# A hybrid encoder layer on one Trainium2 core: three instead of two groups of seven products in the second pass of each down projection

## The chip, the cores and the metric

The kernel runs on one core of one Trainium2 chip. The metric is the time of one execution on the device in microseconds, the median of three runs; the profile comes from one profiled execution, recorded by the hardware profiler. Engines are named as the profile names them: PE is TensorE (matmuls; PEld are its weight loads), DVE is VectorE, ACT is ScalarE, POOL is GpSimd, SP is SyncE, which here issues most of the DMAs.

## What is computed

One layer over 256 rows of width 2048, in float32. Two half feed-forward blocks (FFNs) with an inner width of 5632 stand around a mixer (a state-space part and an attention part), and a gated embedding follows:

```python
def swiglu(h, w_gate, w_up, w_down):
    return (jax.nn.silu(h @ w_gate) * (h @ w_up)) @ w_down

x = x + 0.5 * swiglu(rms_norm(x, ffn1_norm[i]), ffn1_w_gate[i], ffn1_w_up[i], ffn1_w_down[i])
...
x = x + mixed @ w_out[i]
x = x + 0.5 * swiglu(rms_norm(x, ffn2_norm[i]), ffn2_w_gate[i], ffn2_w_up[i], ffn2_w_down[i])
gate = jax.nn.sigmoid(rms_norm(x, ple_norm[i]) @ w_ple_gate[i])
```

The change is in the products with `w_down` (5632 x 2048), once in each FFN; the profile calls the weights `in_ffn_w_down`.

## The kernel before

**Arithmetic.** Each float32 operand of a matmul is split into a high part (`hi`, rounded to the type that PE takes in one pass) and a low part (`lo`, the rest). A product is the sum of three: high by high, low by high, high by low. The split of a weight tile of 128 x 1024 (`split`, lines 181 and 184) is a cast on ACT and a subtraction on DVE. Tiles named `whi`/`wlo` and `shi`/`slo` are two rings of buffers for split weights, 4 and 3 deep, used in turn (`weight_pair`, line 285); `hhi`/`hlo` and `nhi`/`nlo` are split activations.

**Tiling of the down projection** (`ffn`, from line 667). The 5632 rows of `w_down` are 11 k blocks (0 to 10) of 512; the 2048 columns are four blocks of 512, worked off as two pairs (`for n in range(0, ND, 2)`). The 256 rows of x are two tiles of 128. For one k block and one pair there are two ways to multiply:

- *A column, `"c"`* (`Seven.column`, line 543): for each of the two column blocks, both row tiles by the four 128-row parts of the k block, 24 matmuls of 512 columns each, 48 in all. Its weights come in two loads of 1 MB and make four splits.
- *A group of seven products, `"s"`* (`Seven.chunk`, line 505): the same four quarter products by seven instead of eight half-size ones (the Winograd form of Strassen's scheme), 7 x 6 = 42 matmuls. It needs sums of the weight quarters: t1, t2 and t4 are DVE additions of 128 x 1024 (line 502), and a fourth sum is made by a DMA issued by POOL that adds one quarter of the weights onto another in place (line 526). It splits seven weight tiles. It also needs sums of the hidden rows, which `sum_forms` (line 450) makes with four small DVE additions (line 459) and one split.

`plans` (line 693) writes out by hand in which order the k blocks of each pair are taken. `"a"` takes all the k blocks that it lists for the first column block, calls `end(0)`, then takes them in reverse order for the second column block and calls `end(1)`. `end` adds the finished sums into x (line 678) and puts off `nxt.block`, which turns that block of x for the next stage. After the last group, `opened` (line 680) adds the parts that are shared by both columns into x.

**Hidden rows.** `kept` (line 699) holds the two k blocks of split hidden rows used last; any other k block is split again when it is needed. `summed` (line 706) holds the sums of k blocks 1 and 2 from the first pair for the second, but not those of k block 0.

**Turned blocks of x.** The next stage needs x transposed. `Normed.block` (line 388) does it for one block of 512 columns: two transposes of 32 x 32 squares on DVE (line 217), 16 small copies on SP's queue (line 230, `h<-mid`), and then `parted`, which multiplies by the norm's gain and splits (lines 192 and 194). The last block of the mixer's norm goes over PE instead.

**What sets the order.** The program is traced in order. Work that stands beside the matmuls is put off by a number of steps with `put_off`; a step is one weight half (or, in a group, two products) of the traced matmuls. The framework then places the instructions of each engine by its own model of their times, an instruction traced earlier going first among those that are ready. So a number of steps sets a rank and is no wait on the chip. Each engine runs its own list in order.

**Buffers.** Weight loads have five buffers of 1 MB; x occupies two of them, so three are left during the down stage. A buffer is free again when its parts are split. Sums of weights and of hidden rows share two buffers (`sum`).

Of the kernel before, what the change touches and what calls it, by code (L numbers as in the profile page):

```python
# [33 lines left out]
def layer_kernel(ctx: ExitStack, tc: tile.TileContext, a: dict, shapes: dict, out: bass.AP):  # L34
# [10 lines left out]
    ND = D // NB  # L45
# [17 lines left out]
    def uid(s):  # L63
        count[0] += 1
        return f"{s}_{count[0]}"
# [4 lines left out]
    def com(tag):  # L70
        return get(comp, tag, *{"sg": (1024, 1), "h": (1024, 2), "sq": (NB, 1), "mid": (2048, 1)}[tag])
# [4 lines left out]
    def aux(s="aux"):  # L76
        return auxp.tile([P, 1024], F32, tag="aux", name=uid(s))
# [4 lines left out]
    def small(n=8):  # L82
        return smp.tile([P, 8], F32, tag="sm", name=uid("sm"))[:, :n]

    def halves(kind):

        return [
            actp.tile([P, 4, T], F32R, tag=kind + s, name=uid(kind + s), bufs={"n": 4, "h": 2}[kind])
            for s in ("hi", "lo")
        ]  # L90
# [4 lines left out]
    def start(g):  # L95
        beside.append(g)
        return g
# [10 lines left out]
    def put_off(steps, fn, *args):  # L108


        def g():
            for _ in range(steps):
                yield
            fn(*args)

        return start(g())

    def pin(ins):
        return tc.keep_in_program_order(ins)
# [58 lines left out]
    def split(hi, lo, src, scale=None, pinned=False):  # L178

        if scale is None:  # L180
            copy = nc.scalar.copy(hi, src)  # L181
            if pinned:
                pin(copy)
            rest = nc.vector.tensor_tensor(out=lo, in0=src, in1=hi.bitcast(F32), op=ALU.subtract)  # L184
            return copy.ins, rest.ins
        else:
            split_each(hi.unsqueeze(1), lo.unsqueeze(1), src.unsqueeze(1), [scale])
# [27 lines left out]
    def turn_blocks(mid, src, t, k0, nk):  # L215

        nc.vector.transpose(
            mid[:, :, t, k0 : k0 + nk, :].rearrange("p q f b -> p f q b"),
            src.rearrange("p (f q b) -> p f q b", f=nk, q=4),
        )  # L220

    def turn_quarters(out, mid, steps):


        def g():
            for _ in range(steps):
                yield
            for i in range(4):
                for q in range(4):
                    nc.sync.dma_start(  # L230
                        out[32 * q : 32 * q + 32].rearrange("p (t i w) -> p t i w", t=TT, i=4)[:, :, i],
                        mid[32 * i : 32 * i + 32, q].rearrange("p t f b -> p t (f b)"),
                    )
                yield

        return start(g())

    def by_tile(out, nk):

        return out.rearrange("p (x f b) -> p f x b", f=nk, b=32)  # L240
# [53 lines left out]
    @contextmanager  # L294
    def sums_phase(name):
        with phase(name) as pool:
            yield pool
            ring[0] = None
# [76 lines left out]
    class Normed:  # L375
# [12 lines left out]
        def block(self, n):  # L388
            if self.laid:
                ps = self.laid(n)  # L390
            elif n < self.early:

                if n % 2 == 0 or self.mid is None:
                    self.mid = com("mid")
                mid = self.mid[:, n % 2 * 1024 : n % 2 * 1024 + 1024].rearrange(
                    "p (q t f b) -> p q t f b", q=4, t=TT, b=32
                )
                out = com("h")
                for t in range(TT):
                    turn_blocks(mid, xt[t][n], t, 0, 4)  # L400
                soon = n == ND - 1
                turn_quarters(out, mid, 4 if soon else 6)
                put_off(9 if soon else 11, self.parted, n, by_tile(out, 4))
                put_off(1, self.squares, n)
                return
            else:
                ps = aux()
                for t in range(TT):
                    for j in range(4):
                        pin(nc.tensor.transpose(  # L410
                            ps[:, j * T + t * P : j * T + (t + 1) * P], xt[t][n][:, j * P : (j + 1) * P], ident
                        ))
            self.parted(n, ps.rearrange("p (j s) -> p j s", j=4))
            if not self.laid:
                put_off(1, self.squares, n)
# [34 lines left out]
    def sum_forms(pool, u, kind="n"):  # L450

        sums = pool.tile([P, 2, NB], F32, tag="sum", name=uid("rows"), bufs=2)
        s = sums.rearrange("p j n -> p (j n)").rearrange("p (z j x b) -> p z j x b", z=4, j=2, b=32)
        (a11, a21), (a12, a22) = ([u[:, k : k + 2, 4 * t : 4 * t + 4] for t in range(TT)] for k in (0, 2))
        for z, (x, y, op) in enumerate((
            (a21, a22, ALU.subtract), (s[:, 0], a11, ALU.subtract),
            (a11, a21, ALU.subtract), (a12, s[:, 1], ALU.add),
        )):
            nc.vector.tensor_tensor(out=s[:, z], in0=x, in1=y, op=op)
        both = halves(kind)  # L460
        split(*both, sums.rearrange("p j n -> p (j n)").rearrange("p (z t) -> p z t", z=4))
        return both
# [95 lines left out]
    def ffn(i, xn, nxt, bg=None):  # L558
# [4 lines left out]
        sevens = pools.enter_context(sums_phase(f"sums{i}"))  # L563
# [20 lines left out]
        for f in range(NF):  # L584
# [6 lines left out]
            if f >= early:  # L591
# [17 lines left out]
                s = Seven(xn, lambda kb: sums[kb], ((wg, f * NB), (wu, f * NB)), sevens, turns)  # L609
# [59 lines left out]
        def rows(k):  # L669
            return hT[k // 2][:, k % 2 * 4 : k % 2 * 4 + 4]  # L670
# [6 lines left out]
        def gather(x, ps, scale):  # L677
            nc.vector.scalar_tensor_tensor(out=x, in0=ps, scalar=scale, in1=x, op0=ALU.mult, op1=ALU.add)

        def opened(s, n):  # L680
# [11 lines left out]

        plans = (
            (("c", 3), ("c", 4), ("s", 0), ("c", 5), ("c", 6), ("s", 1), ("c", 7), ("c", 8), ("s", 2), ("c", 9), ("c", 10)),
            (("c", 10), ("c", 9), ("s", 2), ("c", 3), ("s", 1), ("a", (0, 4, 5, 6, 7, 8))),
        )
        parts, forms = {}, {}

# [12 lines left out]
        for n in range(0, ND, 2):  # L711

            def end(side):
                m = n + side
                for t, z in enumerate(((2, 4), (3, 8))[side]):
                    gather(xt[t][m], s.bank(z), 0.5)
                put_off(0 if m == ND - 1 and m < nxt.early else 2, nxt.block, m)

            s = Seven(kept, summed, ((wd, n * NB), (wd, (n + 1) * NB)), sevens, turns)
            plan = plans[n // 2]  # L720
            left = sum(kind == "s" for kind, _ in plan)
            for kind, kb in plan:
                final = (kind, kb) == plan[-1]
                if kind == "s":
                    left -= 1
                    s.chunk(kb, () if left else shared)
                    if not left:
                        put_off(0, opened, s, n)
                    continue
                for side in range(2):  # L730
                    s.column(side, (kb,) if kind == "c" else kb[:: 1 - 2 * side], final)
                    if final:
                        end(side)
# [694 lines left out]

    n1, nm, n2, npl = Normed("ffn1_norm", load_turned), Normed("mix_norm"), Normed("ffn2_norm", kinds="hhnn", late=0), Normed("ple_norm", late=0)
    ffn(1, n1, nm, s5_prep)  # L1430

    w_in = a["w_in"][0]
# [47 lines left out]
    mix.close()  # L1480

    ffn(2, n2, npl)


# [43 lines left out]
    n = ND - 1  # L1528
# [12 lines left out]
    s = small(1)  # L1541
# [144 lines left out]
```

## Time and profile before

| what | value |
|---|---|
| median of three runs | 1823.55 us (1822.76 to 1824.12) |
| the profiled execution's own time | 1823.55 us |
| its span, first to last instruction | 1821.8 us |
| PE busy, matmuls | 1814.3 us, 8948 |
| DVE busy, instructions | 1523.6 us, 1779 |
| ACT busy, instructions | 1048.4 us, 1223 |
| POOL busy | 102.6 us |
| moved by DMA | 425.79 MB, mean 234 GB/s |

Times in the profile are microseconds from the start of the span; a duration called "ns" is in nanoseconds. A line such as `L184 DVE TENSOR_TENSOR wlo<-raw,whi` names the line of the kernel, the engine, the operation, and what it writes from what it reads, without buffer numbers. In a timeline the first number is the start, the second the duration, and brackets at the end give the idle time ahead of it and what ended that. Many operations belong to helpers, so one line serves all stages; the stage is told by the time.

The down projection of the first FFN lies roughly between 477 and 711 us, that of the second between 1482 and 1714 us. The output projection (`w_out`), which also turns blocks of x, lies ahead of 1030 us.

### The profile page before, as it was taken

The page shows a single profiled execution, that of the slowest core. Times are in us where ns is not written, and L with a number is a line of the kernel's source. Part 1 is how long each engine was busy: PE and PEld are TensorE (multiplying, and loading weights), DVE is VectorE, ACT ScalarE, POOL GpSimd, SP SyncE. Part 2 cuts the span into 40 slices and gives each one's busy share as a digit, 9 for nine tenths or more (in the row PEclk, how much of TensorE's full clock was granted, in tenths as well). Part 3 has the DMA queues.
Part 4 walks back from the last instruction along what each step waited for, and adds up shares of the span by engine and source line. Part 5 has one row for each costly group of instructions (what it writes and reads, how often), then busy time and mean ns, then how long its engine had stood idle before and what let it go on. Part 6 is the DMA issues. An engine that isn't in the chain of part 4 may idle for free.

```text
span 1821.8 us, 24173 instructions
## 1 busy us (share of the span) xinstructions
PE 1814.3 (100%) x8948; PEld 1503.3 (83%) x8948; DVE 1523.6 (84%) x1779; ACT 1048.4 (58%) x1223; POOL 102.6 (6%) x157
## 2 busy tenths in 40 slices
PE   9999999999999999999999999999999999999998
PEld 7888888888888888888898888888888888888887
DVE  8976769999998885697567899999999999888565
ACT  7544446556565665465685566555565556556554
POOL 0010000000000001010021000000000000000000
PEclk9999999999999999999999999999999999999999
DMA  9699878687877677675636787787778787667563
GB/s 340 233 309 292 252 218 248 219 263 225 259 254 232 187 253 226 182 254 163 218 135 225 230 291 224 262 256 247 232 231 247 236 268 244 229 197 253 171 217 127
DMA packets 234551, 425.79 MB, mean 234 GB/s; under 512 B 24288, under 2 KB 48256, under 8 KB 234272
## 3 DMA queue, kind: packets, MB, share of 16 engines
q1 hardware_dynamic: 223872, 390.06, 64.3%
q0 software_dynamic: 9840, 32.78, 8.2%
q8 instruction: 70, 1.15, 0.3%
q10 hardware_dynamic: 720, 1.41, 0.2%
q14 instruction: 49, 0.40, 0.1%
HBM read 372.41 MB, written 10.88 MB: 210 GB/s over the span
## 4 chain that ended last, share of the span: by engine, by line
PE 95%; SPq 1%; DMA 1%; ACT 1%; DVE 1%; issue 0%; ACTq 0%; DVEq 0%
PE acc L323 17%; PE acc L324 17%; PE acc L328 17%; PE aux L324 6%; PE aux L328 6%; PE aux L323 6%; PE acc L498 4%; PE acc L496 4%; PE acc L495 4%; PE aux L498 3%; PE aux L496 3%; PE aux L495 3%; SPq L1192 1%; DMA raw<-in_w_in 1%; SPq L230 1%; PE aux L1146 0%
## 5 line engine op out<-in xcount | busy, mean ns | idle before, releaser
L184 DVE TENSOR_TENSOR wlo<-raw,whi 128x1024 fp32r<-128x1024 f32 x485 | 587.8, 1224 | 172.2 <-ACT whi L181 171.3
L181 ACT CAST whi<-raw 128x1024 fp32r<-128x1024 f32 x485 | 503.4, 1050 | 330.0 <-PE acc L324 225.8
L323 PE MATMUL acc<-whi,nhi 128*128 128x512 f32 x1036 | 406.7, 393 | 0.7 <-ACT whi L181 0.4
L324 PE MATMUL acc<-whi,nlo 128*128 128x512 f32 x1036 | 403.7, 390 | 0.0
L328 PE MATMUL acc<-wlo,nhi 128*128 128x512 f32 x1036 | 284.0, 389 | 0.0
L184 DVE TENSOR_TENSOR slo<-raw,shi 128x1024 fp32r<-128x1024 f32 x181 | 220.1, 1216 | 21.4 <-ACT shi L181 20.1
L323 PEld LDWEIGHTS acc<-whi,nhi 128*128 128x128 f32 x1036 | 194.8, 188 | 43.4 <-ACT whi L181 1.4
L181 ACT CAST shi<-raw 128x1024 fp32r<-128x1024 f32 x181 | 190.0, 1050 | 67.4 <-DMA raw<-in_ffn_w_down 22.8
L328 PEld LDWEIGHTS acc<-wlo,nhi 128*128 128x128 f32 x1036 | 194.4, 188 | 40.8 <-DVE wlo L184 0.4
L324 PEld LDWEIGHTS acc<-whi,nlo 128*128 128x128 f32 x1036 | 194.9, 188 | 39.5
L181 ACT CAST whi<-sum 128x1024 fp32r<-128x1024 f32 x68 | 71.6, 1053 | 132.0 <-DVE sum L502 114.7
L181 ACT CAST shi<-sum 128x1024 fp32r<-128x1024 f32 x55 | 58.0, 1054 | 100.0 <-DVE sum L502 97.6
L502 DVE TENSOR_TENSOR sum<-sum,raw 128x1024 f32<-128x1024 f32 x82 | 100.0, 1219 | 0.8
L526 POOL DMA_DIRECT2D raw<-raw x41 | 35.5, 866 | 947.7 <-DVE sum L502 662.2
L184 DVE TENSOR_TENSOR wlo<-sum,whi 128x1024 fp32r<-128x1024 f32 x68 | 83.0, 1220 | 3.8 <-ACT whi L181 3.1
L184 DVE TENSOR_TENSOR slo<-sum,shi 128x1024 fp32r<-128x1024 f32 x55 | 67.1, 1220 | 1.0 <-ACT shi L181 0.5
L324 PE MATMUL aux<-whi,hlo 128*128 128x512 f32 x164 | 63.9, 390 | 0.4 <-DVE hlo L184 0.4
L323 PE MATMUL aux<-whi,hhi 128*128 128x512 f32 x164 | 63.8, 389 | 0.0
L323 PE MATMUL acc<-whi,hhi 128*128 128x512 f32 x164 | 63.8, 389 | 0.0
L324 PE MATMUL acc<-whi,hlo 128*128 128x512 f32 x164 | 63.8, 389 | 0.0
L323 PE MATMUL aux<-whi,nhi 128*128 128x512 f32 x152 | 59.1, 389 | 0.0
L324 PE MATMUL aux<-whi,nlo 128*128 128x512 f32 x152 | 59.1, 389 | 0.0
(375 smaller groups left out, 3223.9 us busy)
## 6 DMA issues: line engine op xcount, KB each, us to landing
raw<-in_ffn_w_up SPq DMA_DIRECT2D x88, 1024.0 KB, 5.9
raw<-in_ffn_w_down SPq DMA_DIRECT2D x88, 1024.0 KB, 5.2
raw<-in_ffn_w_gate SPq DMA_DIRECT2D x86, 1024.0 KB, 7.7
raw<-in_w_in SPq DMA_DIRECT2D x32, 1024.0 KB, 5.9
raw<-raw POOLq DMA_DIRECT2D x41, 512.0 KB, 5.4
raw<-in_w_out SPq DMA_DIRECT2D x16, 1024.0 KB, 5.1
raw<-in_w_ple_gate SPq DMA_DIRECT2D x16, 1024.0 KB, 5.2
hT<-mid SPq DMA_DIRECT2D x160, 64.0 KB, 4.8
```

What stands on the lines that cost most here:

```text
L181: copy = nc.scalar.copy(hi, src)
L184: rest = nc.vector.tensor_tensor(out=lo, in0=src, in1=hi.bitcast(F32), op=ALU.subtract)
L230: nc.sync.dma_start(out[32 * q : 32 * q + 32].rearrange("p (t i w) -> p t i w", t=TT, i=4)[:, :, i], mid[32 * i : 32 * i + 32, q].rearrang ...
L323: nc.tensor.matmul(ps[t], lhsT=lh, rhs=hi[:, j, cols], start=start and j == 0, stop=False)
L324: nc.tensor.matmul(ps[t], lhsT=ll, rhs=hi[:, j, cols], start=False, stop=False)
L328: nc.tensor.matmul(ps[t], lhsT=lh, rhs=lo[:, j, cols], start=False, stop=stop and j == 1)
L495: nc.tensor.matmul(ps, lhsT=lh[j], rhs=hi[:, j], start=begin and j == 0, stop=False)
L496: nc.tensor.matmul(ps, lhsT=ll[j], rhs=hi[:, j], start=False, stop=False)
L498: nc.tensor.matmul(ps, lhsT=lh[j], rhs=lo[:, j], start=False, stop=z in final and j == 1)
L502: nc.vector.tensor_tensor(out=t, in0=x, in1=y, op=ALU.add)
L526: nc.gpsimd.dma_start(b12, b22, accum_op=ALU.add)
L1192: nc.sync.dma_start(zt[0][p1 : p1 + HC, z], sv[p0 : p0 + HC, r % 2 * 2 + r // 2])
```

## The change

Three edits.

1. `plans`, second pair: k block 0 is taken out of the `"a"` part and becomes a third group. The order was c10, c9, s2, c3, s1, a(0, 4, 5, 6, 7, 8). It becomes c10, c9, s2, c3, s1, f0, c4, s0, a(5, 6, 7, 8). The new kind `"f"` only makes the sums of hidden rows of its k block, ahead of the group that uses them. This is done in both FFNs.
2. `end`: block `ND - 2`, that is the third block of x (block 2), is turned with `put_off(0, ...)` and no longer `put_off(2, ...)`.
3. `Normed.block`: for blocks 2 and 3 that are turned by DVE, the copies are put off by 4 steps and `parted` by 9; that was so for block 3 alone, and block 2 had 6 and 11. It holds for every norm that turns its blocks in this way, so also for the second FFN's norm, whose blocks are turned during the output projection.

```diff
-                soon = n == ND - 1
+                soon = n >= ND - 2
                 turn_quarters(out, mid, 4 if soon else 6)
                 put_off(9 if soon else 11, self.parted, n, by_tile(out, 4))
...
         plans = (
...
-            (("c", 10), ("c", 9), ("s", 2), ("c", 3), ("s", 1), ("a", (0, 4, 5, 6, 7, 8))),
+            (
+                ("c", 10), ("c", 9), ("s", 2), ("c", 3), ("s", 1), ("f", 0), ("c", 4), ("s", 0), ("a", (5, 6, 7, 8)),
+            ),
         )
...
-                put_off(0 if m == ND - 1 and m < nxt.early else 2, nxt.block, m)
+                put_off(0 if m == ND - 2 or m == ND - 1 and m < nxt.early else 2, nxt.block, m)
...
             for kind, kb in plan:
                 final = (kind, kb) == plan[-1]
+                if kind == "f":
+                    forms[kb] = sum_forms(sevens, rows(kb))
+                    continue
```

## The prediction, made before the result was known

> **What bounds the kernel now.** I read the busy times at the head of the page first, then TensorE's (PE's) waits, then the order of its instructions.
>
> ```profile
> span 1821.8 us, 24173 instructions
> ...
> PE 1814.3 (100%) x8948; PEld 1503.3 (83%) x8948; DVE 1523.6 (84%) x1779; ACT 1048.4 (58%) x1223; POOL 102.6 (6%) x157
> ```
>
> ```profile
> PE aux L324 <- DVE hlo L184: 0.4, 1, 0.4
> PE acc L323 <- ACT whi L181: 0.4, 1, 0.4
> PE aux L498 <- DVE wlo L184: 0.2, 1, 0.2
> ```
>
> PE is busy for the whole span and hardly ever waits; the reader is to see that almost nothing but fewer matmuls can shorten this kernel. "Busy" alone does not prove it, since matmuls overlap, so the timeline of PE has to show how often one starts. These are the first matmul of the seventh product of a group and the first one after the group:
>
> ```profile
> 643.17 0.39 PE L495 MATMUL aux<-whi,nhi 128*128 128x512 f32 x1
> ...
> 644.53 0.39 PE L323 MATMUL acc<-whi,hhi 128*128 128x512 f32 x1
> ```
>
> A product is six matmuls (lines 495 to 498), so one costs (644.53 - 643.17) / 6 = 0.2267 us from start to start; the 0.39 is its length with overlap.
>
> Counting 48 matmuls for a plain k block (both columns) and 42 for a group places the second pair in the trace. In down stage 1 its group on k block 1 ends at 644.53, the "a" part's first column runs to 677.17 and its second to 710.54. In down stage 2 the same points are 1648.79, 1681.49 and 1714.30. The windows view gives, per stretch, its length and the busy time of PE, weight loads, DVE, ACT and POOL, then the granted clock:
>
> ```profile
> 624.13:644.53 20.40, 20.40 (x92) 16.90 (x90) 20.33 (x23) 13.53 (x15) 0.87 (x1) 1.00 0.71 222
> 644.53:677.17 32.64, 32.64 (x146) 27.04 (x144) 27.48 (x28) 18.86 (x20) 0.00 (x0) 1.00 0.74 252
> 677.17:710.54 33.37, 32.94 (x146) 26.96 (x145) 19.45 (x20) 16.23 (x22) 5.75 (x8) 1.00 0.63 188
> 1628.39:1648.79 20.40, 20.40 (x92) 16.89 (x90) 20.33 (x23) 13.64 (x16) 0.86 (x1) 1.00 0.72 217
> 1648.79:1681.49 32.70, 32.70 (x146) 26.96 (x144) 27.73 (x28) 18.94 (x20) 0.00 (x0) 1.00 0.72 255
> 1681.49:1714.30 32.81, 32.81 (x145) 26.96 (x144) 20.16 (x21) 16.92 (x22) 0.00 (x0) 1.00 0.54 177
> ```
>
> Two things matter. While a plain block and a group follow each other (first and fourth row), DVE is busy for all of the time: only the splits that it has done ahead keep PE fed. And the last column should take 6 x 24 x 0.2267 = 32.64 us; it takes 33.37 and 32.81, so 0.73 and 0.17 us are lost there.
>
> **The change, part by part.** *The third group.* k block 0 leaves the "a" part and becomes a group: 42 matmuls instead of 48. That is 6 x 0.2267 = 1.36 us a stage, **2.72 us** for the two, if PE stays fed.
>
> The Trainium skill (TensorE: Matmul & The Clock Gate, Back-to-back issue gap) gives about 131 ns for a sustained 512-column matmul; the 227 ns above speak against it here. By the page twelve matmuls would be worth 1.57 us, and the trace decides.
>
> What it costs the others:
>
> ```profile
> L184 DVE TENSOR_TENSOR wlo<-raw,whi 128x1024 fp32r<-128x1024 f32 x6 | 7.3, 1218 | 0.1
> ...
> L502 DVE TENSOR_TENSOR sum<-sum,raw 128x1024 f32<-128x1024 f32 x2 | 2.4, 1222 | 0.0
> ```
>
> ```profile
> L459 DVE TENSOR_TENSOR rows<-hT x12: 412/418/425, 457.6 to 1531.7; 128x256 f32<-128x256 f32 x12
> ```
>
> DVE gets three sums and seven splits for four splits, so six operations more. "f" adds four small sums of 0.418 and one split, 2.9 us. In return k blocks 0 and 4 are each split from the turned hidden rows once and no longer twice, since the column that runs backwards keeps only its two last blocks: two operations fewer. Net 4 x 1.22 + 2.9 = 7.8 us of DVE a stage. ACT gets three casts and one for "f" less two, about 2 us. DVE has 32.64 - 27.48 + 33.37 - 19.45 = 19.1 us idle behind the old groups, so over the pass there is room; the question is only whether the new group's splits come in time.
>
> The pattern before it answers that: the old pair c3, s1 has the same PE work (20.40 us) as the new pair c4, s0. In s1 the tightest split is that of t4, the second "slo<-sum" below, against PE's low-half matmul of that product:
>
> ```profile
> 630.65 1.23 DVE L184 TENSOR_TENSOR slo<-sum,shi 128x1024 fp32r<-128x1024 f32 x1
> ...
> 635.39 1.22 DVE L184 TENSOR_TENSOR slo<-sum,shi 128x1024 fp32r<-128x1024 f32 x1
> ```
>
> ```profile
> 640.00 0.61 PE L498 MATMUL acc<-slo,hhi 128*128 128x512 f32 x2
> ```
>
> It ends at 636.61, 3.39 us early. From there to the same point of s0, PE takes 20.40 us. DVE has 4 weight splits, 10 of the group's operations and 2 splits of hidden rows, 16 x 1.22 = 19.5 us, and 2.9 for "f" if none of that falls into earlier idle time: 22.4. The lead shrinks by 2.0 us at most and 1.4 are left. If "f" is put behind s1, its cast on ACT waits for its four sums, c4's casts queue behind it, and PE waits for those; that is inside the 2.9. The additions into x (from line 680) that follow s1 move behind s0 and have the same column after them. So I take **0** for stalls in the group; the bounds are 0 and the 4.7 us a stage of the second rival.
>
> The group's DMAs: its two loads replace the two of block 0, and one accumulating DMA is added on POOL.
>
> ```profile
> raw<-in_ffn_w_down SPq DMA_DIRECT2D x88, 1024.0 KB, 5.2
> ...
> raw<-raw POOLq DMA_DIRECT2D x41, 512.0 KB, 5.4
> ```
>
> It has to land between t1 and the seventh product, as in the 41 groups there are; POOL is idle, so it costs nothing unless t1 is late.
>
> *The turned block.* Its wait of two steps is an order of tracing. In the trace the first transpose of block 2 already runs as soon as its rows are there, and the 16 copies follow at once:
>
> ```profile
> 677.14 0.71 DVE L217 STREAM_TRANSPOSE mid<-x 128x512 f32<-128x512 f32 x1
> ```
>
> ```profile
> 680.21 7.91 SPq L230 DMA_DIRECT2D h<-mid  x12
> 688.23 0.52 SPq L313 DMA_DIRECT2D raw<-in_w_in  x1
> ```
>
> What follows from them is the loss of 0.73:
>
> ```profile
> 696.59 0.91 ACT L192 ACTIVATE nhi<-h,gains 128x256 fp32r<-128x256 f32 x2 [5.02 <-DMA h<-mid]
> 697.40 1.03 ACT L181 CAST hhi<-hT 128x1024 fp32r<-128x1024 f32 x1
> ```
>
> ```profile
> 699.75 0.50 PE L324 MATMUL aux<-whi,hlo 128*128 128x512 f32 x1 [0.43 <-DVE hlo L184]
> ```
>
> ACT, in order, sits 5.02 us in front of the block's scaling and only then casts the hidden rows of k block 4, which PE needs. After the change no hidden block is split again that late: the backward column is 8, 7, 6, 5, and 5's cast is due once 8 and 7 are through, 2 x 24 x 0.2267 = 10.9 us behind the column's start, well ahead of the block's scaling (19.4 us behind it, 696.59 - 677.17). So the **0.73 + 0.17 = 0.90 us** go; bounds 0 and 0.90. What could be late next is block 2 itself: the shorter column starts at 710.54 - 0.73 - 1.36 - 21.8 = 686.7 and ends at 708.4; the block is scaled at 686.7 + 19.4 = 706.1, and w_in needs it after two quarters of weights, at 708.4 + 10.9 = 719.3. 13 us cover it, and in stage 2, whose next stage takes the first two quarters of two column blocks first, 24. The two steps themselves (5.4 us) I cost at 0: the cover is larger than they are.
>
> *The same wait in the output projection.* `soon` also holds for block 2 of the second FFN's norm. There the tracing order did bind on SP's queue: its last four copies stand behind the loads of the first group.
>
> ```profile
> 1023.79 0.53 SPq L512 DMA_DIRECT2D raw<-in_ffn_w_gate  x1
> 1027.06 0.37 SPq L512 DMA_DIRECT2D raw<-in_ffn_w_up  x1
> 1027.48 14.70 SPq L230 DMA_DIRECT2D h<-mid  x16
> ```
>
> ```profile
> 1035.81 1.22 DVE L502 TENSOR_TENSOR sum<-raw,raw 128x1024 f32<-128x1024 f32 x1
> ```
>
> ```profile
> 1081.86 0.39 PE L496 MATMUL aux<-whi,nlo 128*128 128x512 f32 x1
> 1082.44 0.73 PE L498 MATMUL aux<-wlo,nhi 128*128 128x512 f32 x2 [0.19 <-DVE wlo L184]
> 1083.02 0.39 PE L323 MATMUL acc<-shi,nhi 128*128 128x512 f32 x1
> ```
>
> Two steps earlier they go ahead of those loads, which come 4 x 0.66 = 2.6 us later (7.91 / 12 each); the second then lands near 1027.06 + 2.6 + 5.2 = 1034.9, still before the sum at 1035.81. The block's scaling comes earlier and may free DVE enough to end the wait at 1082.44, worth up to 0.48 us (three starts take 1083.02 - 1081.86 = 1.16 there instead of 0.68). I take 0; the bounds are that gain and a loss of the same size, if the later loads push DVE's work on instead.
>
> **Sum.** -2.72 - 0.90 + 0 = -3.62 us on the profiled execution, which took 1823.55 us (span 1821.8 and 1.75 around it) and is itself the median of the three runs: **1819.9 us**, 0.2% faster. A measurement of this kernel tells about 0.2% (3.65 us) from no change, so the forecast lies on that edge.
>
> **Rivals.**
> *DVE sets the pace locally.* If a group whose stretch fills DVE (20.33 of 20.40) saves no time, PE waits out what it saves, 1.36 us a stage; only the 0.90 stays: 1822.7 us. For it speaks the lead of 1.4 us; against it that PE was busy for all 20.40 us of that stretch.
> The Trainium skill (Perfetto Trace Analysis, Identifying the Most-Contended Engine and Optimization Strategy) says to judge TensorE's room not by matmul busy time, and each regime by its own most contended engine. By that rule DVE counts here and the group pays nothing; the gapless starts of PE in the same stretch side with the matmuls so far.
> *The weight buffers (slower).* Only three of five are free for weights while x is held. If "f" runs ahead of c4's splits (2.9 us), c4's buffers come free late, and with one load's landing (5.2) on top, t1 and t4 lag 8.1 us behind s1's pattern; 3.4 are covered, so PE stalls 4.7 us a stage: 1819.9 + 9.4 = 1829.3 us. It ends slower than before from a lag of about 5.2 us on. Against it: in the old pair the second load, issued at the end of the row below, is in near 626.5, well before its first use.
>
> ```profile
> 616.74 4.89 SPq L512 DMA_DIRECT2D raw<-in_ffn_w_down  x2
> ```
>
> *The turned block's wait does nothing, and the stall stays.* ACT may still stand before the copies with block 5's cast behind it: -2.72 alone, 1820.8 us.
> *More than the sum.* The wait at 1082.44 goes as well: 1819.9 - 0.48 = 1819.4 us.
>
> **Chances and range.** Forecast 0.45 (half of it on either side of the edge), the stall stays 0.10, DVE's pace 0.18, buffers 0.12, more than the sum 0.15. Faster by over 0.2%: 0.15 + 0.23 = 0.38; slower by over 0.2%: the buffers, 0.12; the rest, 0.50, lies within. The range goes from 1818.9 (all bounds at their best and half a microsecond of spread, the three runs lie within 1.4) to 1823.6 (DVE's pace with half a microsecond more a stage), and leaves out the buffers and little else.
>
> **What would show it.** Right: 12 matmuls fewer; in each second pair three runs of 42 matmuls, starts 0.227 us apart; the last columns 21.8 us long with no wait on a hidden-row split; t4's split of the third group ending over 1 us before its matmul. Wrong: PE waits on "slo" or "wlo" between 655 and 665 us or 1660 and 1670 us; ACT or DVE idle there for a load; the first sum of the third group later than its load; PE waiting for the scaled block 2 in the next stage; new waits after 1030 us.

## The result and the profile after

| | before | after |
|---|---|---|
| median of 21 runs each | 1823.58 us (1822.36 to 1824.68) | 1820.08 us (1819.51 to 1822.08) |
| profiled execution | 1823.55 us | 1820.08 us |
| its span | 1821.8 us | 1818.3 us |

The ratio is 0.9984, with a 95% interval of 0.9978 to 0.9989. The change saves 3.50 us; the forecast was 3.62.

The head of the page of the kernel after, then PE's waits:

```profile
span 1818.3 us, 24176 instructions
...
PE 1810.1 (100%) x8936; PEld 1500.1 (82%) x8936; DVE 1536.4 (84%) x1797; ACT 1051.6 (58%) x1227; POOL 104.1 (6%) x159
```

```profile
PE acc L323 <- ACT whi L181: 0.8, 2, 0.4
PE acc L323 <- ACT whi L274: 0.8, 1, 0.8
PE acc L498 <- DVE slo L184: 0.3, 1, 0.3
```

Twelve matmuls fewer, as the code says. The wait on a hidden-row split (`hlo`, 0.4 us) of before is gone. New are one of 0.3 us on a group's `slo`, a second one of 0.4 on an ACT cast (`whi`, line 181), and one on the cast of line 274. The last costs nothing: it stands in the first 8 us, where other starts come earlier, and by 17 us PE is 0.17 us ahead of before.

Where the 3.50 us came from is read off the ends of the stages. The windows view of the kernel after, cut at c3+s1, c4+s0 and the two last columns of each stage (length, then busy time of PE, weight loads, DVE, ACT, POOL, granted clock, DMA):

```profile
623.96:644.36 20.40, 20.40 (x91) 16.89 (x90) 20.34 (x24) 14.49 (x16) 0.88 (x1) 1.00 0.66 202
644.36:664.76 20.40, 20.40 (x91) 16.89 (x90) 18.56 (x17) 11.95 (x14) 0.87 (x1) 1.00 0.70 217
664.76:686.52 21.76, 21.76 (x97) 18.02 (x96) 20.73 (x23) 12.74 (x13) 0.00 (x0) 1.00 0.72 256
686.52:708.28 21.76, 21.76 (x97) 18.02 (x96) 14.09 (x17) 11.06 (x16) 1.81 (x1) 1.00 0.59 192
1626.50:1646.90 20.40, 20.40 (x91) 16.89 (x90) 20.33 (x23) 13.71 (x15) 0.86 (x1) 1.00 0.61 189
1646.90:1667.30 20.40, 20.40 (x91) 16.89 (x90) 19.71 (x20) 11.56 (x13) 0.89 (x1) 1.00 0.70 221
1667.30:1689.06 21.76, 21.76 (x97) 18.02 (x96) 20.72 (x21) 13.79 (x15) 0.00 (x0) 1.00 0.84 292
1689.06:1710.82 21.76, 21.76 (x97) 18.02 (x96) 11.98 (x14) 10.26 (x16) 0.00 (x0) 1.00 0.61 200
```

Every stretch has exactly the length that its matmuls ask for: 90 starts of 0.2267 are 20.40 us, 96 are 21.76. From the first cut to the end, stage 1 takes 708.28 - 623.96 = 84.32 us where before it took 710.54 - 624.13 = 86.41; stage 2 takes 84.32 for 85.91. That is 2.09 + 1.59 = 3.68 us, and the sum of the prediction for the same stretches is 2.72 + 0.73 + 0.17 = 3.62. Outside, the part ahead of the first cut is 0.17 us shorter (624.13 to 623.96), the part between the stages is 0.37 longer (917.85 to 918.22), and the end is the same to 0.02. So the gain is where it was forecast, and 0.20 us are lost elsewhere.

The 0.37 between the stages is mainly three things. A start in the mixer, where the code is untouched, is 0.53 us late at 894.21; before, at 896.21, it was 0.27 late. The wait at 1082.44, where two starts were 0.47 us late together, has gone. A new one in the first group of the second FFN makes two starts 0.59 us late. DVE and PE there after:

```profile
1043.01 1.22 DVE L444 TENSOR_TENSOR whole<-hhi,hlo 128x1024 f32<-128x1024 f32 x1
1044.15 1.22 DVE L184 TENSOR_TENSOR slo<-sum,shi 128x1024 fp32r<-128x1024 f32 x1
```

```profile
1045.42 0.73 PE L498 MATMUL acc<-slo,hhi 128*128 128x512 f32 x2 [0.32 <-DVE slo L184]
```

Line 444 does not work on the turned block: it adds up the two parts of block 1, for the sums of its rows. But with block 2 turned earlier, its scaling on DVE (line 194) is over by 1037 us, where it ran from 1039 to 1047 before, and line 444 has moved from 1058.91 to 1043.01. It now stands in front of the group's split, and PE waits for that split.

Next, the place where the 0.73 us were lost, on ACT:

```profile
697.60 1.05 ACT L181 CAST hhi<-hT 128x1024 fp32r<-128x1024 f32 x1 [2.12 <-PE aux L328]
703.94 0.51 ACT L192 ACTIVATE nhi<-h,gains 128x256 fp32r<-128x256 f32 x1 [5.28 <-DMA h<-mid]
```

ACT still sits 5.28 us in front of the turned block (5.02 before). But the last cast of hidden rows now stands ahead of that wait and no longer behind it, so PE does not notice.

Last, the new group's own chain. DVE's part of it, PE's matmul that needs the tightest split (t4's), and the group's second weight load on SP's queue:

```profile
642.93 1.22 DVE L184 TENSOR_TENSOR slo<-raw,shi 128x1024 fp32r<-128x1024 f32 x1
...
649.38 1.23 DVE L502 TENSOR_TENSOR sum<-raw,raw 128x1024 f32<-128x1024 f32 x1 [0.69 <-DMA raw<-in_ffn_w_down]
...
655.22 1.22 DVE L502 TENSOR_TENSOR sum<-sum,raw 128x1024 f32<-128x1024 f32 x1
657.55 1.23 DVE L184 TENSOR_TENSOR wlo<-sum,whi 128x1024 fp32r<-128x1024 f32 x1 [1.12 <-ACT whi L181]
```

```profile
660.23 0.61 PE L498 MATMUL acc<-wlo,hhi 128*128 128x512 f32 x2
```

```profile
644.23 0.37 SPq L512 DMA_DIRECT2D raw<-in_ffn_w_down  x1
```

The split ends at 657.55 + 1.23 = 658.78, which is 1.45 us ahead of PE; that is its lead. The forecast was at least 1.4. But DVE waited: 0.69 us for the load and 1.12 us for ACT's cast. The load goes out at 644.23, just behind the end of DVE's split of a raw weight (642.93 + 1.22 = 644.15), which frees a buffer. So here the lead is not set by DVE's sum of work, as the prediction reckoned it, but by a chain: DVE's split frees a buffer, the load takes 5.1 us (644.23 to the sum at 649.38), then come sum, sum, cast, split.

### The profile page after: what moved, and what is told of

The parts are those of the page before. It is cut to its first block, busy times and chain, and to the rows that moved or that the text cites. A ratio compares the mean times of both kernels' runs of the same rounds, so it can differ in the third digit from the quotient of the medians.

```text
span 1818.3 us, 24176 instructions
## 1 busy us (share of the span) xinstructions
PE 1810.1 (100%) x8936; PEld 1500.1 (82%) x8936; DVE 1536.4 (84%) x1797; ACT 1051.6 (58%) x1227; POOL 104.1 (6%) x159
## 4 chain that ended last, share of the span: by engine, by line
PE 94%; DMA 2%; ACT 1%; SPq 1%; DVE 1%; issue 1%; DVEq 0%; ACTq 0%
PE acc L323 16%; PE acc L324 16%; PE acc L328 16%; PE aux L328 6%; PE aux L324 6%; PE aux L323 6%; PE acc L498 4%; PE acc L496 4%; PE acc L495 4%; PE aux L498 3%; PE aux L496 3%; PE aux L495 3%; SPq L1197 1%; DMA raw<-in_w_in 1%; DMA raw<-in_w_out 1%
## 5 line engine op out<-in xcount | busy, mean ns | idle before, releaser
L181 ACT CAST whi<-sum 128x1024 fp32r<-128x1024 f32 x72 | 75.8, 1053 | 144.4 <-DVE sum L502 134.3
L502 DVE TENSOR_TENSOR sum<-sum,raw 128x1024 f32<-128x1024 f32 x86 | 104.9, 1220 | 0.8
L184 DVE TENSOR_TENSOR wlo<-sum,whi 128x1024 fp32r<-128x1024 f32 x72 | 87.9, 1221 | 5.0 <-ACT whi L181 4.2
L323 PE MATMUL aux<-whi,hhi 128*128 128x512 f32 x152 | 59.1, 389 | 0.0
L324 PE MATMUL aux<-whi,hlo 128*128 128x512 f32 x152 | 59.1, 389 | 0.0
```

The source lines that it names most:

```text
L323: nc.tensor.matmul(ps[t], lhsT=lh, rhs=hi[:, j, cols], start=start and j == 0, stop=False)
L324: nc.tensor.matmul(ps[t], lhsT=ll, rhs=hi[:, j, cols], start=False, stop=False)
L502: nc.vector.tensor_tensor(out=t, in0=x, in1=y, op=ALU.add)
```

## The experiments

The theory after the result: the group pays its twelve matmuls in full while its chain keeps a lead over PE, and the two last columns lose nothing because no late cast of hidden rows stands behind the turned block. The rivals: the gain comes from the block's earlier steps; the group's stretch is at DVE's pace and the gain is luck. Each kernel was timed beside the kernel before, whose median was 1823.43 (e2 to e5), 1823.78 (e6 to e8), 1823.71 (e9, e10) and 1823.70 us (e11, e12).

| kernel | median, us | ratio to before, 95% interval |
|---|---|---|
| after | 1820.08 | 0.9984 (0.9978 to 0.9989) |
| e2, earlier steps alone | 1824.78 | 1.0008 (1.0000 to 1.0017) |
| e3, k block 0 plain | 1823.69 | 1.0000 (0.9991 to 1.0009) |
| e4, no early sums | 1821.39 | 0.9988 (0.9979 to 0.9997) |
| e5, no plain block ahead of the group | 1825.50 | 1.0013 (1.0004 to 1.0022) |
| e6, a fourth group in the first pair | 1819.83 | 0.9981 (0.9972 to 0.9990) |
| e7, two more sums | 1823.47 | 1.0000 (0.9991 to 1.0009) |
| e7, five more sums | 1830.46 | 1.0038 (1.0026 to 1.0051) |
| e8, old steps in the output projection | 1820.89 | 0.9985 (0.9976 to 0.9994) |
| e9, the four groups early | 1821.54 | 0.9987 (0.9978 to 0.9996) |
| e10, e9 with the old steps of e8 | 1821.79 | 0.9988 (0.9979 to 0.9997) |
| e11, e6 without the early sums of block 0 | 1818.72 | 0.9979 (0.9970 to 0.9988) |
| e12, e6 without early sums | 1817.93 | 0.9971 (0.9960 to 0.9982) |

### The steps alone (e2)

The kernel before with the two edits of the steps and its old plan.

```diff
 # against the kernel before
-                soon = n == ND - 1
+                soon = n >= ND - 2
...
-                put_off(0 if m == ND - 1 and m < nxt.early else 2, nxt.block, m)
+                put_off(0 if m == ND - 2 or m == ND - 1 and m < nxt.early else 2, nxt.block, m)
```

> Only the two edits to the turned block's wait, on the old plan. If the steps are a rank and nothing more (my theory), the median stays within 0.5 us of the kernel before, the waits of PE near 699.7 and 1703.5 us stay, and only the one behind the output projection may move. If the gain came from the turned block's earlier place (rival), 1 to 3.5 us of the 3.5 come back here without any third group.

It is 1.35 us above before (1824.78 - 1823.43), at the edge of its interval; less than 0.5 was expected. The wait at 699 us is gone in stage 1, but a larger one came in stage 2, and another in the first group of the second FFN. PE's waits there, then SP and ACT ahead of the first one:

```profile
1704.89 0.51 PE L324 MATMUL aux<-shi,hlo 128*128 128x512 f32 x1 [0.95 <-DVE hlo L184]
```

```profile
1047.45 0.73 PE L498 MATMUL acc<-slo,hhi 128*128 128x512 f32 x2 [0.87 <-DVE slo L184]
```

```profile
1684.64 10.99 SPq L230 DMA_DIRECT2D h<-mid  x16
1695.73 4.86 SPq L313 DMA_DIRECT2D raw<-in_w_ple_gate  x3
```

```profile
1701.39 1.05 ACT L181 CAST whi<-raw 128x1024 fp32r<-128x1024 f32 x1 [1.65 <-DMA raw<-in_w_ple_gate]
1702.34 1.05 ACT L181 CAST hhi<-hT 128x1024 fp32r<-128x1024 f32 x1
```

All 16 copies now go out in one run, and the next stage's load behind them goes at 1695.73. In the kernel before it went after the twelfth:

```profile
1684.53 8.59 SPq L230 DMA_DIRECT2D h<-mid  x12
1693.22 0.54 SPq L313 DMA_DIRECT2D raw<-in_w_ple_gate  x1
```

In e2 ACT has the cast of that load in front of the cast of the hidden rows, waits 1.65 us for it, and PE waits for the hidden rows. So on the old plan the steps end the wait of stage 1 and bring larger ones elsewhere; in the total they bring nothing. They are however a condition of the new plan. Counted in the code from the end of the column before, `parted` of block 2 is traced at the 15th step with the old numbers, at the 13th with either edit alone and at the 11th with both. The last column had six k blocks, 12 steps, and has four, 8 steps; `w_in` asks for the block 4 steps behind it, so at the 16th step before and at the 12th after. Only with both edits is the block there in time; no run has the new plan without them.

### The plan without the group (e3)

```diff
 # against the kernel after
-("f", 0), ("c", 4), ("s", 0), ("a", (5, 6, 7, 8))
+("c", 4), ("c", 0), ("a", (5, 6, 7, 8))
```

> The changed kernel with k block 0 as a plain block (c4, c0) in the place of f0, c4, s0: 12 matmuls more, all else as changed. My theory: the two last columns still lose nothing, so it stands 12 x 0.2267 = 2.7 us above the changed kernel and about 0.8 us below the kernel before (1822.8). Rival, the group's splits cost what its matmuls save: no slower than the changed kernel, 1820 to 1820.6.

It is level with before (1823.69 for 1823.43), 0.9 above what was expected, and 3.6 us above after; twelve matmuls account for 2.72 of that. Its two last columns lose nothing: PE is busy for the whole of both rows, and no start in them is late.

```profile
644.40:688.00 43.60, 43.60 (x194) 36.09 (x193) 32.48 (x32) 23.31 (x23) 0.00 (x0) 1.00 0.70 240
688.00:710.00 22.00, 22.00 (x99) 18.22 (x98) 12.69 (x15) 10.21 (x15) 4.64 (x8) 1.00 0.53 151
```

So the 0.90 us are gained at their place here too, without the group. The steps are in this kernel as well, so it does not tell them from the shorter last part. The gain does not arrive in the total of the profiled execution, because other late starts came: 0.57 us at 1368.57, in a stage that no edit touches, and 0.65 us more than before in the first 470 us.

### The early sums (e4) and the plain block between the groups (e5)

```diff
 # e4, against the kernel after
-("f", 0), ("c", 4), ("s", 0)
+("c", 4), ("s", 0)
 # e5, against the kernel after
-("f", 0), ("c", 4), ("s", 0)
+("f", 0), ("s", 0), ("c", 4)
```

> The changed kernel without the separate step f0, so the sums of hidden rows are traced behind c4, with the group itself. My theory: the sums cost 2.9 us of DVE in either place and the cover is 1.4 us or more, so the median stays within 0.5 us of the changed kernel (1820.1). Rival, the place of f decides whether the group is fed: PE waits at the start of the third group, 1 to 3 us a stage, 1822 to 1826.

> The third group straight behind the second, the plain block after it: f0, s0, c4. Same matmuls. My theory: DVE's lead is what feeds a group; without the plain block's 10.9 us of PE, DVE is 3.9 us short per stage (11 operations of 1.22 against 9.5 us of PE) and 6.8 with f, against a lead of 3.4, so PE waits 0.5 to 3.4 us a stage: 1821 to 1827. If DVE's lead does not matter (rival), it stays at 1820.1.

Without the early sums the group does not stall. On the contrary: its second load goes out earlier and t4's lead is larger. The load, t1, and t4's split:

```profile
642.45 0.37 SPq L512 DMA_DIRECT2D raw<-in_ffn_w_down  x1
```

```profile
648.68 1.23 DVE L502 TENSOR_TENSOR sum<-raw,raw 128x1024 f32<-128x1024 f32 x1
...
655.85 1.23 DVE L184 TENSOR_TENSOR wlo<-sum,whi 128x1024 fp32r<-128x1024 f32 x1
```

PE's matmul starts at 660.49, so the lead is 660.49 - 655.85 - 1.23 = 3.41 us instead of 1.45, with the load 1.78 us earlier. Of the 1.96 us that it has grown, only 0.70 come from the load: it has landed at 647.63, and t1 starts when DVE's own list gets to it (648.68 for 649.38). From t1 on DVE does the same number of operations, but a split of a raw weight now stands between t4's sum and its split and fills the time of ACT's cast, where the kernel after has DVE idle for 1.12 us; that gives 1.00. The last 0.26 is PE coming later. A larger lead buys nothing where 1.45 was enough: the time is not better than after. It is 1.3 us above, more than the 0.5 expected, though the intervals lie over each other. The profiled span is 1.0 us longer (1819.3), with a start 0.12 us late on hidden rows at 681.77 and longer waits at 895 and 1046. Why those came is not shown.

Without a plain block between the groups (e5) PE waits in the group, as was expected. In stage 2:

```profile
1654.51 0.50 PE L495 MATMUL aux<-shi,nhi 128*128 128x512 f32 x1 [1.28 <-ACT shi L181]
...
1656.79 1.14 PE L498 MATMUL aux<-slo,nhi 128*128 128x512 f32 x2 [1.08 <-DVE slo L184]
```

DVE in the same stretch, first and last of nine operations:

```profile
1647.57 1.22 DVE L502 TENSOR_TENSOR sum<-raw,raw 128x1024 f32<-128x1024 f32 x1
...
1656.65 1.22 DVE L184 TENSOR_TENSOR slo<-raw,shi 128x1024 fp32r<-128x1024 f32 x1
```

Nine starts in a row 1.135 us apart, (1656.65 - 1647.57) / 8, without a gap: here DVE does set the pace, the first rival of the prediction. In the profiled execution, a long one of 1828.06 us, starts of PE that come late add up to 2.3 us in stage 1 and 4.8 in stage 2. Not all of the 4.8 is waiting. Behind the two waits above, the windows view shows a granted clock of 0.52 for 3.5 us:

```profile
1656.79:1660.30 3.51, 3.51 (x9) 2.74 (x10) 3.51 (x4) 3.51 (x5) 0.00 (x0) 0.52 0.31 63
```

The matmuls there start 0.43 us apart instead of 0.227, which adds 1.7 us. So the stage loses more than PE waits. The median, 1825.50 us (1823.42 to 1829.39), is 5.4 above after. The plain block c4 is what keeps this away.

### How much DVE can be given (e7)

The first sum of the third group, t1, is computed several times over, with the same value.

```diff
 # against the kernel after; times is 3 (two more sums) or 6 (five more)
-            t1 = self.add(b11, b12)
+            t1 = self.add(b11, b12, self.times if kb == 0 else 1)
```

> The changed kernel with t1 of the third group added up three times instead of once (the same sum written again), 2 x 1.14 us more DVE ahead of the group's splits. In the changed kernel's trace t1 leads PE by 4.5 us and t4 by 1.45 us in stage 1 and 3.1 in stage 2. My theory: that lead is all that stands between DVE and PE, so 2.3 us cost 0.8 us in stage 1 and nothing in stage 2: 1820.1 to 1821.5. Rival, DVE sets the pace there already: 2.3 us a stage, 1824.7.

> The same with six sums instead of one, 5 x 1.14 = 5.7 us more DVE. My theory: beyond the lead every microsecond is PE's: 5.7 - 1.45 = 4.3 us in stage 1 and 5.7 - 3.1 = 2.6 in stage 2, 1827.0. Rival, the lead is larger than the trace shows since other splits can go first: 1822 or less. Rival, DVE sets the pace already: 11.4 us, 1831.5.

Two more sums cost 3.4 us (1823.47 - 1820.08), where the theory had 0 to 1.4 and the rival 4.6. Five more cost 10.4, where the theory had 6.9 and the rival 11.4. Both lie nearer to the rival. From two to five the time rises by 7.0 us, 3.5 a stage, for three sums of 1.26 us each ((7.53 - 3.74) / 3, from the lengths of the six and of the three sums in the traces): beyond the lead nearly every microsecond is PE's, as the theory said. What it had too large is the lead. In the profiled execution of two more sums (1825.72 us, the longest of its runs), late starts of PE from the third group to the end of the stage add up to 2.2 us in stage 1 and 0.7 in stage 2. Of 2.5 us more in each, 0.3 and 1.8 were covered, not 1.45 and all.

The same profile shows why the lead of 1.45 in stage 1 did not cover more. The load, t1 (three sums), the sum of t4 and its cast, and the PE matmul that waits:

```profile
645.57 0.37 SPq L514 DMA_DIRECT2D raw<-in_ffn_w_down  x1
```

```profile
650.65 3.74 DVE L504 TENSOR_TENSOR sum<-raw,raw 128x1024 f32<-128x1024 f32 x3 [0.61 <-DMA raw<-in_ffn_w_down]
...
659.00 1.22 DVE L504 TENSOR_TENSOR sum<-sum,raw 128x1024 f32<-128x1024 f32 x1
```

```profile
661.35 0.50 PE L496 MATMUL acc<-whi,hhi 128*128 128x512 f32 x1 [1.48 <-ACT whi L181]
```

t4's sum starts 3.78 us later than in the kernel after (659.00 for 655.22). The two sums are only 2.51 of that (3.74 - 1.23); the other 1.27 is t1 starting late (650.65 for 649.38), because the load went out 1.34 us later. DVE's list up to there is in the same order as in the kernel after, but it runs late: t1 of the group before (s1) already waited for its load, as it did not in the kernel after.

```profile
629.02 1.23 DVE L504 TENSOR_TENSOR sum<-raw,raw 128x1024 f32<-128x1024 f32 x1 [0.76 <-DMA raw<-in_ffn_w_down]
```

That load went out at 620.92 and took 8.08 us to land; in the kernel after, it went out at 620.63 and took 5.10. DVE is 0.49 us behind the kernel after ahead of this sum and 1.34 behind it, and still 1.35 behind at the split that frees the third group's buffer. So a load that lands late in one group passes its lag on to the next one through the buffers.

### The output projection (e8)

```diff
 # against the kernel after
-                soon = n >= ND - 2
+                soon = n == ND - 1 or n == ND - 2 and self.gain != "ffn2_norm"
```

> The changed kernel with the old steps (6 and 11) for block 2 of the second FFN's norm alone, which is turned during the output projection. My theory: PE's wait of 0.59 us at 1045 goes and the one of 0.47 at 1082 comes back, so the median stays within 0.5 us of the changed kernel (1820.1). Rival, the shorter wait costs there: 1 us faster, 1819.

The wait at 1045 is gone and the one of before is back:

```profile
1080.99 0.73 PE L498 MATMUL aux<-wlo,nhi 128*128 128x512 f32 x2 [0.23 <-DVE wlo L184]
```

The time is 0.8 us above after with overlapping intervals (0.5 was expected). The earlier block in the output projection trades one wait for another.

### Does it go on? A fourth group (e6, e9 to e12)

```diff
 # e6, first pair, against the kernel after
-("c", 7), ("c", 8), ("s", 2), ("c", 9), ("c", 10)
+("c", 7), ("s", 2), ("f", 8), ("c", 9), ("s", 8), ("c", 10)
 # e9, first pair
+("c", 3), ("c", 4), ("s", 0), ("c", 5), ("s", 1), ("c", 6), ("s", 2), ("f", 8), ("c", 7), ("s", 8), ("c", 9), ("c", 10)
 # e10: e9, and the edit of e8
 # e11: e6 without ("f", 0) in the second pair;  e12: without ("f", 8) too
```

> The changed kernel with one more group, in the first pair: k block 8 is a group there (s2, f8, c9, s8, c10 at the end of that pair). 12 matmuls fewer. My theory: where a plain block stands between two groups, a cycle costs DVE at most 2.0 us of its lead, and the lead there is 5 us or more, so it stands 2.7 us below the changed kernel, about 1817.4. Rival, DVE sets the pace: 1820 or more, with waits of PE on slo or wlo between 565 and 600 us.

> The kernel after with a fourth group (k block 8) in the first pair as in the run before it, but the four groups stand early, each with one plain block behind it, and the two plain blocks 9 and 10 end the pair. If the lead of the splits (what ACT and DVE have done ahead) is one store that is used up over both pairs, two plain blocks before and two after the turn of the pairs (96 + 96 matmuls, 43.5 us) fill it again before the third group of the second pair: 12 matmuls less than after and no wait on a split at 635 to 680 us, 1820.1 - 2.7 = 1817.4 us. If each stretch has only its own lead, the waits come where four groups follow each other with one plain block between, in the first pair (500 to 585 us, and the same of the second FFN), 1 to 3 us a stage, and the time is 1819.5 to 1823.

> The same with the old steps (6 and 11) for block 2 of the second FFN's norm in the output projection. That took the wait at 1045 us away and brought the one at 1081 back, within 0.8 us. So this is expected within 0.8 us of its neighbour of this call; a larger difference of the two, in waits far from 1030 to 1090 us, would show how much waits elsewhere move with an edit that does not touch their stage.

> The kernel with the fourth group in the first pair (k block 8), without the early sums of hidden rows of k block 0 in the second pair. Theory: the lead of the third group is set by its second load, which is issued when DVE's splits free a weight buffer; the early sums stand ahead of those splits, and without them the load was issued 1.8 us earlier (642.45 for 644.23 us) and t4's split had 3.4 us of lead for 1.45. So here the load, issued at 647.14 us with the early sums, goes out 1 to 2 us earlier, the waits of 0.53 and 0.3 us at 659 to 661 us go, and the time is 0.5 to 1.5 us below its neighbour with the early sums (1818.3 to 1819.3). Rival: DVE's busy time over the stage decides and not the order, the early sums only stand elsewhere; then the load or the sums behind it are late all the same, waits of the same size stay at 655 to 685 us, and the time is 1819.8 or more.

> The same without the early sums of k block 8 in the first pair too. By the theory no other than its neighbour where the first pair has no wait (none was seen there with the early sums): within 0.5 us of it. By the rival too. If the fourth group's own load is set in the same way, the first pair's lead grows by 1 to 2 us and the wait of 0.47 us at 639 us, in the second group of the second pair, goes as well: 0.5 us less.

In e6 twelve matmuls more are gone, yet hardly anything of the 2.72 us arrives (1819.83, with runs from 1817.42 to 1823.85). The new group itself is free of waits, also between 565 and 600 us, where the rival had put them. In the profiled execution late starts of PE in the second pair of stage 1 add up to 2.3 us; stage 2 has none there. They stand in three places: in the second group (0.47 us late at 639.30), in the column behind the third (0.37 at 676.99), and in the third group itself:

```profile
647.14 0.37 SPq L512 DMA_DIRECT2D raw<-in_ffn_w_down  x1
```

```profile
659.57 0.50 PE L495 MATMUL acc<-shi,hhi 128*128 128x512 f32 x1 [0.37 <-ACT shi L181]
...
660.83 0.73 PE L498 MATMUL acc<-slo,hhi 128*128 128x512 f32 x2
```

The two starts are 0.53 and 0.23 us late, and the load is 2.91 us later than in the kernel after. e9 gave the lead four plain blocks to recover in between, and the wait moved to the column behind the group:

```profile
676.93 0.50 PE L324 MATMUL acc<-whi,hlo 128*128 128x512 f32 x1 [1.34 <-DVE hlo L184]
```

DVE is full there, as the windows view of 660 to 680 us shows (its 22 operations take 20.00 us):

```profile
660.00:680.00 20.00, 18.66 (x82) 15.11 (x81) 20.00 (x22) 14.31 (x16) 0.00 (x0) 1.00 0.75 257
```

The additions into x of lines 678 to 689 stand among the splits. The same wait stands in stage 2 at 1678.63, and e10 has both, at 677.10 and 1679.67. Neither side of e9's expectation came true: the time is 1821.54 us and not 1817.4, and the first pair, where the other side had put the waits, has none. e10 is within the 0.8 us of e9, but its wait in stage 2 is 1.36 us for 0.54, in a stage that its edit does not touch.

e11 tested the chain. Without the early sums the load should go out 1 to 2 us earlier and the waits at 659 to 661 us should go:

```profile
643.38 0.37 SPq L512 DMA_DIRECT2D raw<-in_ffn_w_down  x1
```

It went out 3.76 us earlier, though it landed only 2.22 earlier (650.15 for 652.37). The split has 0.64 us of lead, and the waits at 659 to 661 us are gone; one of 0.31 us on hidden rows stands at 680.85. The median, 1818.72 (1817.30 to 1827.11), is in the expected range, though its gain over e6 (1.1 us) is not clear of the intervals. e12 is the fastest at 1817.93 us, 0.8 below e11, which is not clear of the intervals either; the wait at 639 us, which its expectation named, is already gone in e11. Its interval overlaps that of after by a little, it has six runs, and its profiled execution took 1821.90, with waits of 0.90 to 1.07 us at 1044, 1046 and 1643 us; so it points to a better version and does not settle one.

The second load of the third group against t4's lead, in stage 1:

| kernel | load issued, us | t4's split ends | PE needs it | lead |
|---|---|---|---|---|
| e4 | 642.45 | 657.08 | 660.49 | 3.41 |
| after | 644.23 | 658.78 | 660.23 | 1.45 |
| e8 | 645.01 | 659.67 | 660.52 | 0.85 |
| e11 | 643.38 | 658.57 | 659.21 | 0.64 |
| e12 | 644.10 | 659.05 | 659.11 | PE 0.07 late |
| e9 | 645.95 | 659.59 | 659.65 | PE 0.23 late |
| e6 | 647.14 | 660.77 | 660.83 | PE 0.23 late, and 0.53 at the product's start |

In after, e6, e8 and e9 t1 starts 5.15 to 5.25 us behind the issue, as the load lands; there the lead moves with the time when the buffer comes free. In e4 DVE's own list is what t1 waits for, and in e11 and e12 the load takes longer (6.78 and 5.94 us, last section). From the start of t1 to the end of t4's split it is 9.40 us in after and e8, where DVE idles 1.12 us for ACT's cast, and 8.4 in the other five, where another split stands in that place. In e9, e11 and e12 PE also comes earlier (659.21 for 660.23 in e11), since the fourth group has saved its matmuls by then. e8 has the same code as after in this stage and the same order of DVE's list, and still 0.6 us less lead: differences of that size between single traces tell nothing of an edit.

## Why the prediction was right, and where it was not

- **Twelve matmuls, 2.72 us: right, and shown.** The third group runs without a late start in both stages, and without the group (e3) the time is back at that of before.
- **The 0.90 us of the last columns: right.** Both columns are 21.76 us long, and the reason is the one given: ACT still waits for the copies, but nothing that PE needs stands behind. The rival in which the stall stays falls. e3 gains it without the group. The steps alone (e2) end the wait of stage 1 and enlarge that of stage 2, so they do not do it; what the shorter last part would do without them is not shown.
- **No stalls in the group: right. The 1.4 us of lead: right by luck.** The sum counted the right operations: from the end of t4's split in s1 (636.33) to that in s0 (658.78) DVE's list has the 17 large ones and three of the four small. But it took each at its length (17 x 1.22 + 4 x 0.418 = 22.4), where operations without a gap start 1.135 us apart (as in the nine starts of e5), and it had DVE never waiting. The trace has 20.64 us of work, not 22.4, and 1.81 us of waiting, 0.69 for the load and 1.12 for ACT. The two errors cancel: 22.45 us for 22.4. The list of signs named the waiting: "ACT or DVE idle there for a load" came true without harm.
- **The two steps at 0: wrong, on their own.** The cover of block 2 was there. But without the steps the new plan would ask for the block before its scaling is traced, so they are no separate term. And the tracing order, though a rank and no wait, decides what stands ahead of what on SP, ACT and DVE: in e2 four copies went past a weight load and PE lost 0.95 us in stage 2, and 0.87 us at 1047. In the kernel after only the smaller wait of 0.32 remains of it.
- **The output projection, 0 with bounds of 0.48 on either side: right.** The wait at 1082.44 goes, one of 0.32 comes at 1045. The mechanism named for the loss, later loads that push DVE's work on, was not it: a sum for block 1's rows (line 444) stands ahead of the split. Of the two loads that the forecast had 2.6 us later, the second goes out at 1025.27 for 1027.06 before, with PE 2.0 us ahead of before there: 0.2 us later.
- **The weight buffers: the mechanism is there, the price was not paid.** The lag eats lead first. In e6, with the load 2.91 us later, the lead is used up and PE's late starts in that pair are 2.3 us, not the 4.7 that this rival had.
- **DVE's pace: not in this change, but near.** Without c4 it sets the pace (e5). With it, DVE's 18.56 and 19.71 of 20.40 us leave room, but little: 2.5 us more of DVE in each of the two groups takes back the whole gain (e7). The Trainium skill (Perfetto Trace Analysis, Optimization Strategy) says that a gap that repeats in a stretch, on the engine that should be saturated, can mean too few buffers for the next tile. The traces have one on DVE and not on PE: 0.6 to 0.8 us of waiting for the load, at the same place of stage 1 in after, e6, e7, e8 and e9. The load goes out 0.07 to 0.08 us behind the split that frees its buffer (644.15 and 644.23 in after), which fits; no run has more buffers.

What stays open: small waits at 894, 1044 to 1047, 1368 and 1643 us come and go from kernel to kernel, up to about a microsecond each, mostly in stages whose code is the same. That one follows the order of a list was seen at 1045 alone. They are why single edits here can't be added up below 1 us.

## What to carry to other kernels

When an engine is busy for the whole span, count its instructions; that gives the gain, and the lead of what feeds it says whether the gain is paid. Price a queue of operations by the distance of their starts, not by their length, and look for the waits inside it. Read that lead at the tightest operand, and follow its chain back to its first link: here a buffer freed by a split, then a load of 5 us, then sums and splits. A second such edit draws on the same lead, so the next group is only free if there is lead left for it. Leaving out the early sums (e11, e12) points that way, without settling it.

## What the runs showed of the hardware beyond that

The same two loads of 1 MB at the same place of the code take up to 2.1 us longer in one kernel than in another. SP's queue at the third group of stage 1, with the view of the group's two loads (time from issue to landing), in the kernel after and then in e11:

```profile
634.89 0.37 SPq L313 DMA_DIRECT2D raw<-in_ffn_w_down  x1
638.97 5.63 SPq L512 DMA_DIRECT2D raw<-in_ffn_w_down  x2
...
DMA to landing us min/median/max: 5.0/5.1/5.1
```

```profile
638.84 0.37 SPq L313 DMA_DIRECT2D raw<-in_ffn_w_down  x1
639.97 3.77 SPq L512 DMA_DIRECT2D raw<-in_ffn_w_down  x2
...
DMA to landing us min/median/max: 6.7/6.7/6.8
```

In e6 the two take 7.2 and 5.2 us. What differs is the load ahead (line 313, a plain block's). In the kernel after, it goes out 4.1 us before the group's first load and has 1.0 us to go; in e11 and e6 it goes out 1.1 us before and has 4 us to go. Over all loads of `in_ffn_w_down` in the fourteen traces, the time to landing grows with what the load ahead still has to go: a median of 5.1 us where that is under 1 us, 6.6 at 3 to 4 us, 8.0 at 5 to 6. So most of the spread goes with loads that overlap. The spread is as large as the lead of the new group, 1.45 us, so a lead of this size is no safe one. The accumulating DMA of each group never showed as a wait in the groups read here; its median from issue to landing went from 5.4 to 5.9 us for 41 and 43 of them.
